# Input sums at every fifth place between matmuls, and wider steps in loading head outputs, in a two-layer decoder trunk

## The chip, the core and the metric

The kernel runs on one core of a Trainium2 chip. TensorE multiplies matrices into PSUM banks, VectorE, ScalarE and GpSimd work element by element, and SyncE issues the loads of the weights. The metric is the device time of one execution in microseconds, the median of three runs. Less is better.

## The reference, cut to what is computed

Two layers of a decoder trunk for 512 tokens of width 1024, all in float32:

```python
p      = x @ W_in        # retention q/k/v/gate, mLSTM q|k/v/o/i/f, two merge gates gA, gB
y_A    = P_A( swish(g_ret) * HeadNorm(Retention(q,k,v)) )
y_B    = P_B( sigmoid(o) * HeadNorm(mLSTM(conv(q),conv(k),v,i,f)) )
x      = LN(alpha * x + W_out( sigmoid(gA) * y_A + sigmoid(gB) * y_B ))
x      = LN(alpha * x + SwiGLU(x))
```

Retention and mLSTM have four heads each, with queries and keys of 128 columns and values of 256. The retention's score of two tokens is damped by their distance, its queries and keys are rotated by their position, and both branches normalise each head's output.

## The kernel before

**Numbers in two parts.** Each float32 operand is kept as a rounded part (`...h`, or `whi` for a weight) and the remainder that the rounding left (`...l`, `wlo`). A product is three matmuls: rounded by rounded, rounded by remainder, remainder by rounded. ScalarE makes the rounded parts (weights at L201), VectorE the remainders (`lo_of`, L133, for weights, values, scores and all else).

**Units.** The weights come in units of 512 KB, loaded by SyncE into `wraw`. A unit is 24 matmuls of 512 columns in the projections, or 24 of 256 columns in the quads, and its preparation runs up to four units ahead (`prep_to`, `used`). PSUM has four banks for projections (`pm`) and four for the rest (`pa`).

**The layer.** In a layer come two pairs of retention heads, two pairs of mLSTM heads, four quads (two for each merge gate), the branch outputs, W_out, the norm and SwiGLU. A retention pair (the loop over `p`, L665 on) is: four projections for queries and keys, each taken out of PSUM by a rotation (`rot_evac`: three VectorE products at L607 to L609, one GpSimd add at L610); the value projection, whose four banks become `rvh` on ScalarE and `rvl` on VectorE (`v_evac`); and the gate projection.

**Quads.** A quad makes four blocks of a projection from seven units instead of eight. It needs sums of weights (VectorE L187 to L191, GpSimd L223) and sums of blocks of the layer's input. `input_sums` (L571) makes the latter in four parts `m`: two GpSimd adds (L577) join rounded part and remainder of two blocks into a scratch tile `xs`, four VectorE operations (L583) fill a scratch tile `sf`, ScalarE rounds it to `xs0h` (L585; `xs1h` in layer 1), VectorE makes the remainder `xs0l` (L133). The results are not read before the quads.

**Work between matmuls.** TensorE's and SyncE's orders are written out by hand. Work beside the unit that is running is kept as generators in a queue `side`; `slot()` (L244) steps the first of them on and is called between matmuls (four times in a projection by units of features, sixteen in one by tokens, twice in a unit of a quad). For the second pair the queue holds the first pair's `head_norms` (which writes the head outputs `ot` to memory, `od`, at L543) during the rotations, and from then on the first head's `scores`, `input_sums`, and after the value projection `weighted`, the second head's `scores` and `weighted`. On VectorE, ScalarE and GpSimd a scheduler places the instructions; in the quads their order is as written, too.

**Head outputs.** `fetch` (L546) loads them back in four parts: GpSimd issues the load into a scratch tile `of` (L550), ScalarE rounds it to `orh` (L554), VectorE makes `orl`. The first `fetch` stands beside quads three and four, the second one (`om0h`, `om0l`) behind it, beside the next projection. All scratch tiles (`xs`, `sf`, `of`, `ot`, the quads' `ga` and `gc`, the scores' `pf` and `qf`) share four buffers.

Of the kernel before, what the change touches and what calls it, by code (L numbers as in the profile page):

```python
# [104 lines left out]
def decoder_trunk(ctx: ExitStack, tc: tile.TileContext, wall, xT_in, x_in, pvec, lnp, rtab, out):  # L105
# [18 lines left out]
    def scratch(shape, name):  # L124
        return reg.tile(shape, F32, tag="sc", name=name, bufs=4)

    def bigpair(which, name):
        h = big.tile([P, KT, S], F32R, tag=f"{which}h", name=f"{name}h")
        l = big.tile([P, KT, S], F32R, tag=f"{which}l", name=f"{name}l")
        return h, l  # L130

    def lo_of(out_lo, full, hi):
        nc.vector.tensor_tensor(out=out_lo, in0=full, in1=hi.bitcast(F32), op=ALU.subtract)  # L133
# [4 lines left out]
    for l in range(L):  # L138
        i = 0
        while i < NUNIT:  # L140
            n, m = len(loads), l * NUNIT + i
# [97 lines left out]
        prep_to(state["used"] + LOOK)  # L239


    side = deque()

    def slot():  # L244
        while side:
            try:
                next(side[0])
                return
            except StopIteration:
                side.popleft()  # L250

    def drain():
        while side:
            slot()
# [18 lines left out]
    def feat_if(xh, xl, evac):  # L273

        w = take()
        pm = main_bank()
        hi = w[0].rearrange("p (k m) -> p k m", k=KT)
        for k in range(KT):
            nc.tensor.matmul(pm, lhsT=hi[:, k], rhs=xh[:, k], start=(k == 0), stop=False)
            nc.tensor.matmul(pm, lhsT=hi[:, k], rhs=xl[:, k], start=False, stop=(k == KT - 1))  # L280
            if k % 4 == 3:
                slot()
        used()
        evac(pm)
# [119 lines left out]
    xh, xl = bigpair("A", "x0")  # L404
# [141 lines left out]
    def fetch(od, his, los):  # L546

        for i in range(4):
            t = scratch([P, 2, S], "of")
            nc.gpsimd.dma_start(t, od[:, 2 * i : 2 * i + 2])  # L550
            yield
            yield
            hi, lo = (x[i // 2][:, 2 * i % 4 : 2 * i % 4 + 2] for x in (his, los))
            nc.scalar.copy(hi, t)  # L554
            yield
            lo_of(lo, t, hi)
            yield
# [10 lines left out]
    def sum_views(which, name):  # L568
        return tuple(t.rearrange("p (s m) (c t) -> p s (m c) t", s=4, c=2) for t in bigpair(which, name))

    def input_sums(xh, xl, sh, sl):  # L571

        t1, t2 = slice(0, S // 2), slice(S // 2, S)
        for m in range(4):
            t = scratch([P, 2, S], "xs")
            for i in range(2):
                nc.gpsimd.tensor_tensor(out=t[:, i], in0=xh[:, m + 4 * i].bitcast(F32), in1=xl[:, m + 4 * i].bitcast(F32), op=ALU.add)  # L577
            yield
            f = scratch([P, 4, S // 2], "sf")
            a11, a12, a21, a22 = t[:, 0, t1], t[:, 1, t1], t[:, 0, t2], t[:, 1, t2]  # L580
            for i, a, b, op in ((0, a21, a22, ALU.subtract), (1, f[:, 0], a11, ALU.subtract),
                                (2, a11, a21, ALU.subtract), (3, f[:, 1], a12, ALU.add)):
                nc.vector.tensor_tensor(out=f[:, i], in0=a, in1=b, op=op)  # L583
            yield
            nc.scalar.copy(sh[:, :, m], f)  # L585
            lo_of(sl[:, :, m], f, sh[:, :, m])
            yield
# [5 lines left out]
    for l in range(L):  # L593
# [7 lines left out]
        xs = sum_views(oth, f"xs{l}")  # L601
        od = [dr.tile([P, KT, S], F32, tag=f"od{i}", name="od") for i in range(2)]

        def rot_evac(dst):
            def ev(pm):
                t = scratch([P, S], "rt")
                nc.vector.tensor_tensor(out=dst, in0=pm, in1=tab[:, 0], op=ALU.mult)  # L607
                nc.vector.tensor_tensor(out=t[0:64], in0=pm[64:128], in1=tab[0:64, 1], op=ALU.mult)
                nc.vector.tensor_tensor(out=t[64:128], in0=pm[0:64], in1=tab[64:128, 1], op=ALU.mult)  # L609
                nc.gpsimd.tensor_tensor(out=dst, in0=dst, in1=t, op=ALU.add)  # L610
            return ev
# [51 lines left out]
            yield  # L663

        for p in range(2):  # L665
            qk = reg.tile([P, 4, S], F32, tag="qk", name="rqk")
            rots = [rot_evac(qk[:, i]) for i in range(4)]
            if p == 0 and l > 0:
# [24 lines left out]
                return mult, key_weight, query_weight  # L693

            side.append(scores(qk, 0, boxes[0], *ret_weights(2 * p)))
            if p == 1:
                side.append(input_sums(xh, xl, *xs))
            if p == 0:
                side.append(rest(12))
                side.append(if_cols())  # L700
# [160 lines left out]

        ordered = {mybir.EngineType.Activation, mybir.EngineType.DVE, mybir.EngineType.Pool}
        with tc.manual_schedule(engines=ordered):
            for m in (0, 4):
                quad(xh, xl, *xs, gate_ev(sga, 0, m))
            drain()
            orh = [reg.tile([P, 4, S], F32R, tag=t, name="orh") for t in ("vh", "vl")]
            orl = [reg.tile([P, 4, S], F32R, tag=t, name="orl") for t in ("gt", "oo")]
            side.append(fetch(od[0], orh, orl))
            for m in (0, 4):  # L870
                quad(xh, xl, *xs, gate_ev(sgb, 8, m))
            drain()
# [245 lines left out]
        if not last:  # L1118
            xh, xl, _ = nxt
# [78 lines left out]
```

## Time and profile before

| what | value |
|---|---|
| median of three runs | 1806.07 us (1804.14 to 1806.31) |
| the profiled execution | 1806.1 us, of which the span is 1804.4 us |
| TensorE busy | 1772.4 us (98%) |
| VectorE busy | 1263.8 us (70%) |
| ScalarE busy | 794.3 us (44%) |
| GpSimd busy | 420.6 us (23%) |

The span runs from the first instruction to the last; busy times are shares of it. In the rows, PE is TensorE, DVE VectorE, ACT ScalarE, POOL GpSimd, SP SyncE, and L with a number is a line of the kernel before. A matmul's own time (0.39 us) overlaps the next one's: the step from start to start is what it costs. TensorE's clock is given as a share of its full speed, 1.00 being 2.4 GHz and 0.50 being 1.2 GHz.

### The profile page before, as it was taken

The numbers are of one execution on the slowest core, as the hardware profiler recorded it, in microseconds if no ns is written. First come the engines' busy times: TensorE is split into PE (matmuls) and PEld (weight loads), VectorE is DVE, ScalarE is ACT, GpSimd is POOL, SyncE is SP. The second block draws the span as 40 slices with busy tenths as digits, with TensorE's granted clock in tenths as the row PEclk, the third lists the DMA queues.
The fourth block names the chain that finished last, engine by engine and source line by source line (L and its number), as shares of the span: only waits on it lengthen the run. The fifth ranks groups of instructions, "written<-read, shape, count | busy, mean of one in ns | idle before, by whom it ended". The sixth has DMA issues, their size and how long they took to land.

```text
span 1804.4 us, 26440 instructions
## 1 busy us (share of the span) xinstructions
PE 1772.4 (98%) x10616; PEld 1580.5 (88%) x10616; DVE 1263.8 (70%) x1686; ACT 794.3 (44%) x1148; POOL 420.6 (23%) x309
## 2 busy tenths in 40 slices
PE   9998999999999999999999999999999999999997
PEld 7887888998889999988898788889988899999886
DVE  6676666775459999963476856667755599999534
ACT  4434655554225444452244345556532254444410
POOL 2041100231001455620120400012310015554200
PEclk9999999999999999999999999999999999999999
DMA  7332322247332333362243233213463333333521
GB/s 247 91 97 94 109 79 94 71 140 248 98 116 89 127 95 101 106 214 94 86 160 94 93 99 112 89 64 117 127 236 101 109 106 94 106 118 106 198 70 47
DMA packets 72826, 209.43 MB, mean 116 GB/s; under 512 B 6616, under 2 KB 8536, under 8 KB 71680
## 3 DMA queue, kind: packets, MB, share of 16 engines
q1 hardware_dynamic: 62864, 168.32, 29.0%
q0 software_dynamic: 9840, 39.43, 6.4%
q8 instruction: 83, 1.36, 0.3%
q14 instruction: 39, 0.32, 0.1%
HBM read 190.93 MB, written 16.79 MB: 115 GB/s over the span
## 4 chain that ended last, share of the span: by engine, by line
PE 92%; DVE 5%; issue 1%; ACT 1%; DMA 1%; POOL 0%; SPq 0%; DVEq 0%; ACTq 0%
PE pm L318 25%; PE pm L351 9%; PE pm L352 8%; PE pm L353 8%; PE pm L262 7%; PE pm L260 7%; PE pm L261 7%; PE pa L318 4%; PE pa L352 3%; PE pa L351 3%; PE pa L353 3%; DVE wlo L133 1%; DVE sf L583 1%; PE pa L484 1%; PE pa L485 1%; PE pa L486 1%
## 5 line engine op out<-in xcount | busy, mean ns | idle before, releaser
L133 DVE TENSOR_TENSOR wlo<-wraw,whi 128x1024 fp32r<-128x1024 f32 (+2 forms) x404 | 569.8, 1423 | 231.3 <-ACT whi L201 228.8
L201 ACT CAST whi<-wraw 128x1024 fp32r<-128x1024 f32 x391 | 408.8, 1049 | 507.2 <-PE pm L261 133.9
L440 POOL TENSOR_TENSOR rs<-ve,nhalf 128x4 f32<-128x4 f32 (+1 forms) x32 | 32.2, 1006 | 525.1 <-DVE ve L439 525.1
L351 PE MATMUL pm<-whi,x0h 128*128 128x512 f32 x256 | 102.9, 402 | 8.2 <-DVE rvl L133 8.1
L351 PE MATMUL pm<-whi,x20h 128*128 128x512 f32 x256 | 103.2, 403 | 7.0 <-DVE rvl L133 7.0
L353 PE MATMUL pm<-wlo,x20h 128*128 128x512 f32 x256 | 100.9, 394 | 0.0
L352 PE MATMUL pm<-whi,x20l 128*128 128x512 f32 x256 | 100.8, 394 | 0.0
L353 PE MATMUL pm<-wlo,x0h 128*128 128x512 f32 x256 | 100.7, 393 | 0.0
L352 PE MATMUL pm<-whi,x0l 128*128 128x512 f32 x256 | 100.5, 393 | 0.0
L223 POOL TENSOR_TENSOR wraw<-wraw 128x1024 f32<-128x1024 f32 x28 | 67.4, 2408 | 110.1 <-issue 54.4
L1049 POOL TENSOR_TENSOR qa<-qa 128x512 f32<-128x512 f32 x20 | 42.8, 2141 | 142.5 <-DVE qa L1048 90.6
L318 PE MATMUL pm<-s1h,wlo 128*128 128x256 f32 x240 | 67.9, 283 | 0.0
L318 PE MATMUL pm<-x10h,whi 128*128 128x256 f32 x240 | 67.9, 283 | 0.0
L318 PE MATMUL pm<-x10h,wlo 128*128 128x256 f32 x240 | 67.9, 283 | 0.0
L318 PE MATMUL pm<-s0h,whi 128*128 128x256 f32 x240 | 67.9, 283 | 0.0
L318 PE MATMUL pm<-x11h,whi 128*128 128x256 f32 x240 | 67.9, 283 | 0.0
L318 PE MATMUL pm<-x10l,whi 128*128 128x256 f32 x240 | 67.9, 283 | 0.0
L318 PE MATMUL pm<-s0l,whi 128*128 128x256 f32 x240 | 67.9, 283 | 0.0
L318 PE MATMUL pm<-x11l,whi 128*128 128x256 f32 x240 | 67.9, 283 | 0.0
L318 PE MATMUL pm<-s1h,whi 128*128 128x256 f32 x240 | 67.9, 283 | 0.0
L318 PE MATMUL pm<-s0h,wlo 128*128 128x256 f32 x240 | 67.9, 283 | 0.0
L318 PE MATMUL pm<-x11h,wlo 128*128 128x256 f32 x240 | 67.9, 283 | 0.0
(511 smaller groups left out, 5573.3 us busy)
## 6 DMA issues: line engine op xcount, KB each, us to landing
wraw<-wall SPq DMA_DIRECT2D x307, 512.0 KB, 3.7
od<-ot POOLq DMA_DIRECT2D x16, 512.0 KB, 3.0
of<-od POOLq DMA_DIRECT2D x16, 512.0 KB, 4.9
gb<-lnp POOLq DMA_DIRECT2D x4, 1024.0 KB, 6.5
x1d<-xr POOLq DMA_DIRECT2D x8, 512.0 KB, 2.9
xr<-x1d POOLq DMA_DIRECT2D x8, 512.0 KB, 4.7
negm<-md POOLq DMA_DIRECT2D x2, 1026.0 KB, 7.1
xr<-xtok POOLq DMA_DIRECT2D x4, 512.0 KB, 6.6
```

What stands on the lines that cost most here:

```text
L133: nc.vector.tensor_tensor(out=out_lo, in0=full, in1=hi.bitcast(F32), op=ALU.subtract)
L201: nc.scalar.copy(hi, sum_t[i])
L223: nc.gpsimd.tensor_tensor(out=raw_t[u + 2], in0=raw_t[u], in1=raw_t[u + 3], op=ALU.add)
L260: nc.tensor.matmul(pm[:, c0:c1], lhsT=hi[:, k], rhs=xh[:, k, c0:c1], start=(k == 0), stop=False)
L261: nc.tensor.matmul(pm[:, c0:c1], lhsT=hi[:, k], rhs=xl[:, k, c0:c1], start=False, stop=False)
L262: nc.tensor.matmul(pm[:, c0:c1], lhsT=lo[:, k], rhs=xh[:, k, c0:c1], start=False, stop=(k == KT - 1))
L318: nc.tensor.matmul(pm, lhsT=x[:, j, k], rhs=y[:, k], start=go and n == 0, stop=j == 1 and k == 3 and n == 2, skip_group_check=not first)
L351: nc.tensor.matmul(pm, lhsT=sh(k)[:, a], rhs=hi[:, j], start=first, stop=False)
L352: nc.tensor.matmul(pm, lhsT=sl(k)[:, a], rhs=hi[:, j], start=False, stop=False)
L353: nc.tensor.matmul(pm, lhsT=sh(k)[:, a], rhs=lo[:, j], start=False, stop=last)
L440: nc.gpsimd.tensor_tensor(out=rs[:, :n], in0=ve[:, :n], in1=nhalf[:, :n], op=ALU.pow)
L1049: nc.gpsimd.tensor_tensor(out=v, in0=v, in1=u, op=ALU.subtract)
```

## The change

A second queue, `slow`, is stepped on at every fifth call of `slot()`. `input_sums` goes into it at the start of the second pair, ahead of the rotations, and no longer into `side` behind the first head's scores. One step within a part of the sums is joined with the one behind it. In `fetch` one more step lies between load and rounding, and one more between rounding and remainder: a part takes six steps instead of four.

```diff
-    side = deque()
+    side, slow = deque(), deque()
+    SLOW = 5
+    turn = {"n": 0}
 
     def slot():
+        turn["n"] += 1
+        if slow and turn["n"] % SLOW == 0:
+            if next(slow[0], "end") == "end":
+                slow.popleft()
         while side:
...
             nc.gpsimd.dma_start(t, od[:, 2 * i : 2 * i + 2])
             yield
             yield
+            yield
             hi, lo = (x[i // 2][:, 2 * i % 4 : 2 * i % 4 + 2] for x in (his, los))
             nc.scalar.copy(hi, t)
+            yield
             yield
             lo_of(lo, t, hi)
             yield
...
                 nc.vector.tensor_tensor(out=f[:, i], in0=a, in1=b, op=op)
-            yield
             nc.scalar.copy(sh[:, :, m], f)
             lo_of(sl[:, :, m], f, sh[:, :, m])
             yield
...
         for p in range(2):
+            if p == 1:
+                slow.append(input_sums(xh, xl, *xs))
             qk = reg.tile([P, 4, S], F32, tag="qk", name="rqk")
...
             side.append(scores(qk, 0, boxes[0], *ret_weights(2 * p)))
-            if p == 1:
-                side.append(input_sums(xh, xl, *xs))
```

An `assert not slow` ahead of the quads is the only other line. In the changed program the lines of `input_sums` stand 8 further down (L577 is L585, L583 is L591), those of `rot_evac` and of the quads 7 (L610 is L617, L843 is L850, L853 is L860), that of the write of head outputs 6 (L543 is L549). What the two programs have in a row, by engine:

GpSimd in layer 0, from the first pair's norms (`rs`) to the end of the second pair's rotations (`rqk`) and the sums' adds (`xs`), before:

```order
L440 TENSOR_TENSOR rs<-ve,nhalf 128x4 x2
L610 TENSOR_TENSOR rqk<-rqk,rt 128x512 x2
L543 DMA od<-ot 128x1024
L610 TENSOR_TENSOR rqk<-rqk,rt 128x512
L543 DMA od<-ot 128x1024
L610 TENSOR_TENSOR rqk<-rqk,rt 128x512
L577 TENSOR_TENSOR xs<-x0h,x0l 128x512 x8
```

GpSimd at the same place, in the changed program:

```order
L446 TENSOR_TENSOR rs<-ve,nhalf 128x4
L585 TENSOR_TENSOR xs<-x0h,x0l 128x512 x2
L446 TENSOR_TENSOR rs<-ve,nhalf 128x4
L617 TENSOR_TENSOR rqk<-rqk,rt 128x512
L585 TENSOR_TENSOR xs<-x0h,x0l 128x512
L617 TENSOR_TENSOR rqk<-rqk,rt 128x512
L585 TENSOR_TENSOR xs<-x0h,x0l 128x512
L549 DMA od<-ot 128x1024
L617 TENSOR_TENSOR rqk<-rqk,rt 128x512
L549 DMA od<-ot 128x1024
L617 TENSOR_TENSOR rqk<-rqk,rt 128x512
L585 TENSOR_TENSOR xs<-x0h,x0l 128x512 x4
```

The first two parts' four adds moved ahead of the third rotation, four stayed behind the fourth; the writes of head outputs keep their places among the rotations, with four adds ahead of them. In layer 1 the first part's two adds stand ahead of the first rotation, the second part's ahead of the third, four behind the fourth.

VectorE in layer 0, the end of the way to the first values' remainders (`rvl`), before:

```order
L583 TENSOR_TENSOR sf<-sf,xs 128x256
L583 TENSOR_TENSOR sf<-xs 128x256
L583 TENSOR_TENSOR sf<-sf,xs 128x256
L133 TENSOR_TENSOR wlo<-wraw,whi 128x1024
L583 TENSOR_TENSOR sf<-xs 128x256
L133 TENSOR_TENSOR xs0l<-sf,xs0h 128x4x256
L583 TENSOR_TENSOR sf<-sf,xs 128x256
L583 TENSOR_TENSOR sf<-xs 128x256
L583 TENSOR_TENSOR sf<-sf,xs 128x256
L133 TENSOR_TENSOR wlo<-wraw,whi 128x1024
L133 TENSOR_TENSOR xs0l<-sf,xs0h 128x4x256
L133 TENSOR_TENSOR rvl<-pm,rvh 128x512 x3
```

VectorE at the same place, in the changed program:

```order
L591 TENSOR_TENSOR sf<-xs 128x256 x2
L591 TENSOR_TENSOR sf<-sf,xs 128x256
L591 TENSOR_TENSOR sf<-xs 128x256
L591 TENSOR_TENSOR sf<-sf,xs 128x256 x2
L591 TENSOR_TENSOR sf<-xs 128x256
L591 TENSOR_TENSOR sf<-sf,xs 128x256
L133 TENSOR_TENSOR xs0l<-sf,xs0h 128x4x256
L133 TENSOR_TENSOR wlo<-wraw,whi 128x1024
L133 TENSOR_TENSOR xs0l<-sf,xs0h 128x4x256
L133 TENSOR_TENSOR wlo<-wraw,whi 128x1024
L133 TENSOR_TENSOR rvl<-pm,rvh 128x512 x3
```

All four parts stood between the fourth rotation and `rvl`; now the first part stands ahead of the fourth rotation, the second part's VectorE work right behind that rotation, and the last two, shown here, where they were. In layer 1 the last part goes behind `rvl`, among the second head's scores.

VectorE in the fourth quad, from the third quad's last take-out (`ga`, L853) on, before:

```order
L853 TENSOR_TENSOR ga<-pm,ga 128x512
L133 TENSOR_TENSOR orl<-of,orh 128x1024
L133 TENSOR_TENSOR wlo<-wraw,whi 128x1024 x4
L843 TENSOR_TENSOR gc<-ga,pm 128x512
L133 TENSOR_TENSOR wlo<-wraw,whi 128x1024
L846 TENSOR_TENSOR ga<-pa,ga 128x512
```

VectorE at the same place, in the changed program:

```order
L860 TENSOR_TENSOR ga<-pm,ga 128x512
L133 TENSOR_TENSOR wlo<-wraw,whi 128x1024
L133 TENSOR_TENSOR orl<-of,orh 128x1024
L133 TENSOR_TENSOR wlo<-wraw,whi 128x1024 x3
L850 TENSOR_TENSOR gc<-ga,pm 128x512
L133 TENSOR_TENSOR orl<-of,orh 128x1024
L133 TENSOR_TENSOR wlo<-wraw,whi 128x1024
L853 TENSOR_TENSOR ga<-pa,ga 128x512
```

One weight's remainder moved ahead of `orl`, and the last `orl`, which was the one behind `ga`, now stands behind the take-out `gc`.

## Rows read from the trace of the kernel before

**Rows 1.** Waits of PE: engine tile line <- releaser: us in total, times, longest

```profile
PE pm L351 <- DVE rvl L133: 15.1, 4, 6.4
PE pa L318 <- DVE wlo L133: 2.8, 2, 1.7
```

**Rows 2.** Timeline of PE: start, us, engine, line, what, [idle before <- releaser]

```profile
140.39 0.39 PE L352 MATMUL pm<-whi,x0l 128*128 128x512 f32 x1
140.62 0.39 PE L353 MATMUL pm<-wlo,x0h 128*128 128x512 f32 x1
147.39 0.79 PE L351 MATMUL pm<-whi,x0h 128*128 128x512 f32 x1 [6.38 <-DVE rvl L133]
...
150.96 0.40 PE L351 MATMUL pm<-whi,x0h 128*128 128x512 f32 x1
...
1032.74 0.39 PE L353 MATMUL pm<-wlo,x20h 128*128 128x512 f32 x1
1039.51 0.80 PE L351 MATMUL pm<-whi,x20h 128*128 128x512 f32 x1 [6.38 <-DVE rvl L133]
...
1044.76 0.40 PE L351 MATMUL pm<-whi,x20h 128*128 128x512 f32 x1
```

**Rows 3.** A window (PE, PEld, DVE, ACT, POOL busy; PEclk; DMA; GB/s), a chain piece

```profile
147.00:148.00 1.00, 0.61 (x2) 0.52 (x3) 1.00 (x3) 1.00 (x2) 0.00 (x0) 0.50 0.76 287
...
577.62 11.52 PE pm L318 x96
```

**Rows 4.** Timelines of DVE, layers 0 and 1, and of POOL (last row)

```profile
119.82 1.23 DVE L133 TENSOR_TENSOR wlo<-wraw,whi 128x1024 fp32r<-128x1024 f32 x1
...
124.07 1.51 DVE L583 TENSOR_TENSOR sf<-xs 128x256 f32<-128x256 f32 x1
...
142.18 1.21 DVE L133 TENSOR_TENSOR xs0l<-sf,xs0h 128x1024 fp32r<-128x1024 f32 x1
143.31 0.41 DVE L583 TENSOR_TENSOR sf<-sf,xs 128x256 f32<-128x256 f32 x1
...
146.65 1.28 DVE L133 TENSOR_TENSOR rvl<-pm,rvh 128x512 fp32r<-128x512 f32 x2
...
1038.78 1.88 DVE L133 TENSOR_TENSOR rvl<-pm,rvh 128x512 fp32r<-128x512 f32 x3
...
119.88 2.31 POOL L610 TENSOR_TENSOR rqk<-rqk,rt 128x512 f32<-128x512 f32 x1 [3.38 <-DVE rt L609]
```

**Rows 5.** Windows of layer 0: L583 on DVE, then all engines

```profile
119.80:146.70 26.90, 11.57 (x16) 0.94 0.21 61
...
66.00:117.00 51.00, 51.00 (x261) 43.21 (x260) 27.21 (x54) 21.79 (x38) 10.14 (x7) 1.00 0.29 89
```

**Rows 6.** Timelines of DVE and PE in layer 1, second head's keys

```profile
1061.18 0.35 DVE L473 SCALAR_TENSOR_TENSOR pp<-pa,pv,pp 128x128 fp32r<-128x128 f32 x1 [0.43 <-ACT pp L472]
...
1062.92 0.28 PE L486 MATMUL pa<-rvh,pp 128*128 128x256 f32 x1
```

**Rows 7.** Timelines in layer 0's fourth quad; page: DMA issues, KB, us to landing

```profile
403.71 1.05 ACT L201 CAST whi<-wraw 128x1024 fp32r<-128x1024 f32 x1 [4.74 <-PE pm L318]
...
407.28 1.05 ACT L554 CAST orh<-of 128x1024 fp32r<-128x1024 f32 x1
...
404.66 0.68 DVE L853 TENSOR_TENSOR ga<-pm,ga 128x512 f32<-128x512 f32 x1
408.36 1.23 DVE L133 TENSOR_TENSOR orl<-of,orh 128x1024 fp32r<-128x1024 f32 x1 [3.02 <-ACT orh L554]
...
404.88 2.39 POOL L223 TENSOR_TENSOR wraw<-wraw 128x1024 f32<-128x1024 f32 x1 [1.86 <-issue]
...
410.77 0.39 PE L318 MATMUL pa<-xs0h,wlo 128*128 128x256 f32 x1 [1.05 <-DVE wlo L133]
...
od<-ot POOLq DMA_DIRECT2D x16, 512.0 KB, 3.0
of<-od POOLq DMA_DIRECT2D x16, 512.0 KB, 4.9
```

More of the change, by code (lines that the diff above doesn't have):

```diff
@@ L863, in decoder_trunk @@
         with tc.manual_schedule(engines=ordered):
+            assert not slow
             for m in (0, 4):
```

## The prediction, made blind

> **What bounds the kernel now.** I read the waits of TensorE first, because TensorE is the only engine that is nearly always at work. Its whole list is short, and two groups of it touch the change [rows 1]: four waits of the matmuls behind a value projection for the values' remainder `rvl` (15.1 us in all, the longest 6.4) and two waits in the quads for a weight's remainder `wlo` (2.8 us in all, the longest 1.7). Everything else on TensorE is matmuls back to back, so the change can only give back these waits, or make new ones. The timeline of TensorE then shows where they lie. In layer 0 the last matmul of the second pair's value projection starts at 140.62 and the next one, due 0.23 us later (the step from 140.39 to 140.62), starts at 147.39; in layer 1 the same two stand at 1032.74 and 1039.51 [rows 2]. Each is a gap of 6.54 us beyond the normal step, and after each the granted clock is at 0.50, the lower level of 1.2 GHz [rows 3].
>
> **What a gap costs with its tail.** In layer 0 the six 512-column and six 256-column matmuls from 147.39 to 150.96 take 3.57 us [rows 2]. At the higher level they take 6 x 0.23 + 6 x 0.12 = 2.10 (0.12 from 96 matmuls in 11.52 us, [rows 3]). The tail is 1.47 us and the gap with its tail 8.0 us. In layer 1 nine and six matmuls take from 1039.51 to 1044.76, 5.25 us against 9 x 0.23 + 6 x 0.12 = 2.79; tail 2.46, together 9.0 us. So 17.0 us lie in the two places.
>
> **Why the gap is there.** Before it VectorE has no idle time: from the last rotation (its first following instruction starts at 119.82) to the first `rvl` at 146.65 it works through weight remainders, the first head's scores and all four input sums [rows 4]. The 16 subtractions of L583 take 11.57 us of that stretch [rows 5], 0.72 each, though one takes 0.41 alone (143.31); the one at 124.07 takes 1.51 [rows 4]. The long ones run while GpSimd makes the sums' adds (L577). So a GpSimd add costs VectorE about 1.1 us (1.51 - 0.41), and there are eight adds in the stretch. It also goes the other way: the rotation's add at 119.88 takes 2.31 us beside a weight remainder at 119.82 that takes its usual 1.23 [rows 4]; there GpSimd waited, not VectorE.
>
> **The sums, layer 0.** A sum is two adds on GpSimd, four subtractions and one remainder on VectorE, and one rounding copy on ScalarE. In the changed order the first sum goes wholly before the fourth rotation, the second keeps its VectorE part behind it, but its two adds go before; the third and fourth stay where all were. The stretch loses on VectorE 4 x 0.41 + 1.21 = 2.85 us (the 1.21 is the `xs0l` remainder at 142.18, [rows 4]), and four adds at 1.1 = 4.4 us of waiting. Against that, the rotation's add now meets the second sum's short subtractions in place of one long weight remainder, so VectorE may wait 1.1 us there. Given back: 2.85 + 4.4 - 1.1 = 6.15. The first `rvl` then starts at 146.65 - 6.15 = 140.5, and TensorE 0.74 after it, as now (147.39 - 146.65): 141.24, against 140.85 due. 0.4 us of gap stay. The bounds: 7.25 without that wait (no gap), and 2.85 if no add's wait is saved; then `rvl` starts at 143.8, a gap of 3.7 us and a tail of at most the 1.5 seen now, 5.2 us lost. I take 0.4, because the waits of 1.1 us are read from rows of this very stretch.
>
> The Trainium skill ("SBUF — State Buffer", section "SBUF: two separate sides") says that VectorE and GpSimd share a pair of ports as an exclusive lock: the one that starts first holds it for its whole instruction and "the other fully blocks"; for a VectorE operation without a faster mode this holds if both inputs lie in SBUF. The rows on 1.51 against 0.41 agree. By this rule moved adds cost their lock again wherever they go, so it speaks against a gain from moving them.
>
> Whether they cost it there depends on how full the new place is. In the stretch from 66 to 117 us VectorE works 27.21 of 51 us and GpSimd 10.14 [rows 5]. What comes in there is one sum on VectorE (2.85), four adds (two sums) and their waits (4.4), and a rounding copy: 7.3 us into 23.8 idle ones. So I cost it at nothing. If that cover were gone, the rotations would come late by as much as 7.3 us, with the scores' matmuls behind them. ScalarE's copy of the first sum stands ahead of a weight copy and of the head outputs' copies; a unit of 24 matmuls lasts 24 x 0.23 = 5.5 us, ScalarE works 21.79 of the 51 [rows 5], and the copy of that shape takes 1.05 [rows 7].
>
> **The sums, layer 1.** Here the first sum goes before the fourth rotation and the fourth goes behind the values, into the gate projection; the adds of the third and fourth stay. The stretch loses 8 x 0.41 + 2 x 1.21 = 5.7 us and 4.4 us of waits. The first `rvl` would start at 1038.78 - 10.1 = 1028.7; it has to start by 1032.97 - 0.74 = 1032.2, so nothing of the gap stays (at the bound of 5.7 alone it starts at 1033.1, 0.9 us late). The fourth sum's 2.85 us now stand between the second head's scores, whose key remainder ends at 1061.18 + 0.35 = 1061.53; the matmul that reads it starts at 1062.92 [rows 6]. Slack 1.4 us, and VectorE idles there between its pieces (0.43 before this very one). Cost between 0 and 2.85 - 1.4 = 1.45 us; I take 0.1.
>
> **The head outputs' loads.** In the fourth gate quad the place of the wait is the weight remainder of its fifth unit. ScalarE has that weight rounded at 403.71 + 1.05 = 404.76, and VectorE is free from 404.66 + 0.68 = 405.34; but in VectorE's order the remainder `orl` of the fourth head output comes first, and waits 3.02 us for its copy on ScalarE (407.28 + 1.05). It runs from 408.36 for 1.23, the weight remainder behind it, and TensorE goes on at 410.77 after 1.05 us idle [rows 7]. In layer 1 the same wait is the longer of the two, 1.7 [rows 1]. With the wider steps the weight remainder stands ahead of that `orl`, so it can start at about 405.4; behind GpSimd's weight sum (2.39 us from 404.88) at the latest at 407.3, to end at 408.5, a good microsecond before it is due. Both waits go: 2.8 us. Bounds: nothing, if something else is late there, to 2.8.
>
> **Sum.** 17.0 - 0.4 - 0.1 + 2.8 = 19.3 us. The profiled execution took 1806.1 us, of which the span is 1804.4; its time is that of the median, 1806.07. So 1806.1 - 19.3 = 1786.8 us. With every term at its best bound 1786.3, at its worst 17.0 - 5.2 - 0.9 - 1.45 = 9.4, 1796.7.
>
> **Rivals.** (a) VectorE's waits for GpSimd come back in layer 0: the moved adds meet VectorE beside the earlier rotations, these come late, and the four adds that stay cost as much as the eight do now. Then only the 2.85 are given back and half of the gap stays. For it speaks that my sum ends within 0.4 us of the due time, with no slack, and that three sums still have their VectorE part ahead of `rvl`; against it the 23.8 idle us of the new place. Time: 1786.8 + (5.2 - 0.4) = 1791.6. It is also what the Trainium skill's rule on the lock ("SBUF — State Buffer", as above) gives where the new place is full.
>
> (b) The wider steps make a new wait behind the fourth quad. Two loads of the second head output now stand behind the fourth load of the first one on GpSimd, and the second of them needs the buffer that the fourth `orl` gives free. The fourth load is issued behind GpSimd's weight sum, at 404.88 + 2.39 = 407.3; with 4.9 to land, a copy of 1.05 and a remainder of 1.23 [rows 7] its `orl` ends at 414.5. The load behind it lands at 419.4, and ScalarE, which takes that copy ahead of the sigmoid that frees a bank of the quad, is held to about 420.5. The bank is wanted by the third unit of the projection behind the quads. TensorE's fifth unit of the quad starts at 410.77; three units of 24 x 0.12 = 2.9 and two of 5.5 later it is 430.5. So it should fit by 10 us. If something on the way is later than these rows say, I price it at the 3 us that `orl` waits now, in each layer, with the 2.8 not gained: 1786.8 + 2.8 + 6 = 1795.6.
>
> (c) Slower. The second sum of layer 0 takes over a buffer from which a head output is written out, and that write is now issued behind more adds on GpSimd, at the latest behind the third rotation's add: a unit of 5.5 us before 119.88 + 2.31 [rows 4], so at 116.7. It lands 3.0 later [rows 7], at 119.7, just ahead of the fourth rotation's last piece. VectorE works in order: if the write lands later, every instruction behind, `rvl` among them, is late by as much. To lose the 19.3 us and 3.6 more each layer must lose 11.5, so it decides from a write that lands at about 131, nearly five times as long as the writes take. Time then: 1812 (each layer 12.5 us late).
>
> (d) The change does not do what it says: TensorE's and SyncE's orders are the same in both programs, only VectorE, ScalarE and GpSimd are re-ordered. If the adds simply wait for buffers and run where they ran, 1803 to 1806.
>
> **How the numbers follow.** A measurement here can tell about 0.2%, 3.6 us, from no change. The forecast has 0.62 (1784.4 to 1789), (a) 0.18, (b) 0.09, (d) 0.06, (c) 0.05. The range reaches from the best bound, 1786.3, less the 1.9 us by which the fastest run shown (1804.14) lies under the median, over (a) with as much to spare on its side: 1784.4 to 1793.5; outside it are (c), (d) and most of (b). Faster by over 0.2%: 0.62 + 0.18 + 0.09 = 0.89; within 0.2%: 0.06; slower: 0.05.
>
> **What would show it.** Right: no wait of TensorE for `rvl` above 1 us in the second pair, no stretch of half clock behind it, no wait in the fourth gate quad; the first `rvl` of layer 0 at about 140.5 and of layer 1, relative to its value projection, some four microseconds before its due time; L583 at a mean well under 0.72 in layer 0. Wrong: `rvl` of layer 0 beyond 142 while VectorE stays without idle time, which is (a); a wait of TensorE in the projection behind the quads, (b); a wait of VectorE's L583 for a write to memory, (c).

## The result, and the profile after

The changed kernel takes 1786.17 us (median of four runs, 1784.78 to 1788.28) against 1805.43 us before (four runs, 1804.14 to 1806.31). The ratio is 0.9895 with an interval of 0.9878 to 0.9912: 1.05% faster. The prediction was 1786.8 us in a range from 1784.4 to 1793.5. The profiled execution has a span of 1786.6 us against 1804.4.

The waits of TensorE in the changed kernel, its whole list (the engine, the tile and the line that waited, what it waited for, us in total, times, the longest):

```profile
PE pm L357 <- DVE rvl L133: 2.3, 2, 1.7
PE pm L344 <- ACT whi L429: 2.3, 1, 2.3
PE pm L401 <- DVE nhalf L403: 1.1, 1, 1.1
PE pm L345 <- DVE wlo L133: 1.0, 2, 0.8
PE pa L667 <- DVE rows L658: 0.2, 1, 0.2
```

Of the four waits for `rvl` in [rows 1] the two long ones are gone; the two that stay are those of the first pairs. The waits of the quads for a weight's remainder (2.8 us in [rows 1]) are gone, and no new group has come.

The timeline of TensorE at the two places of [rows 2], layer 0 and layer 1:

```profile
143.46 0.39 PE L359 MATMUL pm<-wlo,x0h 128*128 128x512 f32 x1
143.69 0.40 PE L357 MATMUL pm<-whi,x0h 128*128 128x512 f32 x1
...
145.79 0.40 PE L357 MATMUL pm<-whi,x0h 128*128 128x512 f32 x1
...
1026.32 0.39 PE L359 MATMUL pm<-wlo,x20h 128*128 128x512 f32 x1
1026.55 0.39 PE L357 MATMUL pm<-whi,x20h 128*128 128x512 f32 x1
...
1028.64 0.40 PE L357 MATMUL pm<-whi,x20h 128*128 128x512 f32 x1
```

The step over the former gap is 0.23 us in both layers, where it was 6.77. From the last matmul of the value projection (143.46) to the one at 145.79 it is 2.33 us, against 10.34 for the same matmuls before (140.62 to 150.96): 8.0 us less in layer 0. In layer 1 the stretch from 1026.32 takes 2.32 us to 1028.64; before, the matmul that answers to the last one started at 1043.52, and the half clock went on to 1044.76 (1029.34 in the changed kernel), so that 9.0 us are saved to there.

The timeline of VectorE on the way to the first `rvl` in layer 0, then that `rvl` in layer 1, then GpSimd's add of the fourth rotation:

```profile
122.67 1.85 DVE L591 TENSOR_TENSOR sf<-xs 128x256 f32<-128x256 f32 x2
...
129.17 0.72 DVE L700 TENSOR_TENSOR qf<-rqk,rtab 128x256 f32<-128x256 f32 x1
129.82 2.31 DVE L133 TENSOR_TENSOR wlo<-wraw,whi 128x1024 fp32r<-128x1024 f32 x1
...
132.78 1.53 DVE L133 TENSOR_TENSOR pp<-qf,pp 128x256 fp32r<-128x256 f32 x1
134.23 1.85 DVE L591 TENSOR_TENSOR sf<-xs 128x256 f32<-128x256 f32 x2
...
142.76 1.88 DVE L133 TENSOR_TENSOR rvl<-pm,rvh 128x512 fp32r<-128x512 f32 x3
...
1023.35 0.68 DVE L133 TENSOR_TENSOR rvl<-pm,rvh 128x512 fp32r<-128x512 f32 x1
...
122.73 1.51 POOL L617 TENSOR_TENSOR rqk<-rqk,rt 128x512 f32<-128x512 f32 x1 [3.40 <-DVE rt L616]
```

The stretch from the fourth rotation to `rvl` takes 142.76 - 122.67 = 20.09 us, where it took 146.65 - 119.82 = 26.83 [rows 4]: 6.74 less. The four rows with 1.85 (two operations), 2.31 and 1.53 are those that a GpSimd add held up by 1.1 us: the rotation's add at 122.67, the sums' adds in the other three. TensorE needs `rvl` started by 143.69 - 0.74 = 142.95; it starts 0.2 us before that.

The window of that stretch with L591 (which was L583) alone; columns as in [rows 5]:

```profile
122.67:142.76 20.09, 6.45 (x12) 1.00 0.24 66
```

Twelve operations at a mean of 0.54 us, where sixteen had 0.72.

The fourth quad of layer 0 on VectorE, then ScalarE, then GpSimd's sum of weights:

```profile
397.75 0.68 DVE L860 TENSOR_TENSOR ga<-pm,ga 128x512 f32<-128x512 f32 x1
398.35 3.12 DVE L133 TENSOR_TENSOR wlo<-wraw,whi 128x1024 fp32r<-128x1024 f32 x1
401.39 1.21 DVE L133 TENSOR_TENSOR orl<-of,orh 128x1024 fp32r<-128x1024 f32 x1
...
416.06 0.83 ACT L840 ACTIVATE sgb<-pm,pv 128x256 f32<-128x256 f32 x2
...
397.97 2.41 POOL L223 TENSOR_TENSOR wraw<-wraw 128x1024 f32<-128x1024 f32 x1 [3.59 <-issue]
```

VectorE goes on without idle time where it waited 3.02 us [rows 7]. The weight remainder takes 3.12 us, since it meets the sum of weights, and is still in time.

**Where the time went.** Both programs give TensorE the same 10616 matmuls in the same order, so the start of each can be set against the start of its twin. The difference, after less before, changes at these places only:

| place | change of the difference, us |
|---|---|
| layer 0, first 62 us | +1.3 |
| layer 0, first pair, behind its own wait for `rvl` | +1.5 |
| layer 0, second pair: gap 6.5, half clock 1.5 | -8.0 |
| layer 0, fourth quad | -1.3 |
| layer 1, second pair: gap 6.5, half clock 2.5 | -9.0 |
| layer 1, quads: 0.4 ahead of the fourth, 2.0 in it | -2.4 |
| sum | -17.9 |

The two spans differ by 17.8. The first two rows are no work of the change, which does nothing before the second pair. They are the clock; those 1.3 us lie in the first 21 us. The windows of the kernel before (as rows 3: PE, PEld, DVE, ACT, POOL busy; PEclk; DMA; GB/s):

```profile
5.00:35.00 30.00, 27.28 (x106) 21.34 (x106) 18.49 (x32) 13.54 (x23) 3.09 (x2) 0.94 0.80 280
...
62.00:75.00 13.00, 12.23 (x67) 10.65 (x68) 7.93 (x18) 3.03 (x7) 0.01 (x1) 1.00 0.37 110
```

and of the changed one:

```profile
5.00:35.00 30.00, 26.67 (x100) 20.83 (x100) 17.13 (x30) 13.37 (x23) 3.09 (x2) 0.89 0.77 270
...
62.00:75.00 13.00, 11.26 (x55) 9.58 (x56) 7.67 (x14) 3.71 (x8) 0.54 (x1) 0.87 0.28 82
```

In the profile of after the granted clock of the first 35 us is 0.89 for 0.94, and the wait of 1.7 us in the first pair, which both kernels have, is followed by half clock in one and not in the other (0.87 for 1.00). Behind the first pair the two profiles differ by 8.0 + 1.3 + 9.0 + 2.4 = 20.7 us. All but the 0.4 ahead of layer 1's fourth quad (see the second run) is the change.

### The profile page after: what moved, and what is told of

Same layout as the page of the kernel before. It is cut to its first block, busy times and chain, and to the rows that moved or that the text cites. A ratio compares the mean times of both kernels' runs of the same rounds, so it can differ in the third digit from the quotient of the medians.

```text
span 1786.6 us, 26435 instructions
## 1 busy us (share of the span) xinstructions
PE 1769.7 (99%) x10616; PEld 1579.3 (88%) x10616; DVE 1269.8 (71%) x1686; ACT 795.4 (45%) x1148; POOL 415.6 (23%) x309
## 4 chain that ended last, share of the span: by engine, by line
PE 95%; DVE 3%; issue 1%; ACT 1%; DMA 1%; SPq 0%; DVEq 0%
PE pm L324 27%; PE pm L357 9%; PE pm L359 9%; PE pm L358 9%; PE pm L268 7%; PE pm L266 7%; PE pm L267 7%; PE pa L324 5%; PE pa L358 3%; PE pa L357 3%; PE pa L359 3%; PE pa L490 1%; PE pa L491 1%; PE pa L492 1%; PE pa L546 1%
## 5 line engine op out<-in xcount | busy, mean ns | idle before, releaser
L133 DVE TENSOR_TENSOR wlo<-wraw,whi 128x1024 fp32r<-128x1024 f32 (+2 forms) x404 | 579.2, 1445 | 230.1 <-ACT whi L201 227.0
L324 PE MATMUL pm<-s1l,whi 128*128 128x256 f32 x240 | 67.9, 283 | 0.0
```

The source lines that it names most:

```text
L324: nc.tensor.matmul(pm, lhsT=x[:, j, k], rhs=y[:, k], start=go and n == 0, stop=j == 1 and k == 3 and n == 2, skip_group_check=not first)
```

## Experiments

**Each part alone.** The first run keeps the sums' new places and takes the old steps in loading; the second does the opposite.

```diff
 # e1_sums_only, against the changed kernel
             nc.gpsimd.dma_start(t, od[:, 2 * i : 2 * i + 2])
             yield
             yield
-            yield
...
             nc.scalar.copy(hi, t)
             yield
-            yield
             lo_of(lo, t, hi)
```

> The input sums go at every fifth place, the loading of head outputs keeps its old steps. Theory (two separate gains that add up): both gaps before rvl in the second pairs are gone, the waits in the fourth gate quads (1.05 and 1.71 us before) stay: 8.0 us less in layer 0, 9.1 less in layer 1, so about 17 us under the kernel before, ratio 0.9905. Rival (the two parts share the gain, since both put off VectorE work): the waits in the quads go too, or part of a gap comes back, and the time is within 1 us of the whole change (ratio 0.9895) or over 0.993.

Measured: 1788.3 us (four runs) against 1804.77, ratio 0.9900 (0.9887 to 0.9913). Its waits of TensorE, the first two groups:

```profile
PE pa L324 <- DVE wlo L133: 2.4, 2, 1.6
PE pm L357 <- DVE rvl L133: 2.3, 2, 1.7
```

The waits in the quads are back (2.4 us, 2.8 before) and the two gaps are gone. Matmul against matmul, the second pairs give 8.0 and 9.0 us. The theory holds, the rival falls.

The second run has the fetch of the changed kernel in the kernel before:

```diff
 # e2_fetch_only, against the kernel before
             nc.gpsimd.dma_start(t, od[:, 2 * i : 2 * i + 2])
             yield
             yield
+            yield
...
             nc.scalar.copy(hi, t)
+            yield
             yield
             lo_of(lo, t, hi)
```

> Only the wider steps in loading head outputs. Theory: the gaps before rvl stay at 6.4 us idle each, the waits in the two fourth gate quads go, 1.2 us in layer 0 and 2.3 in layer 1, so 3.5 us less, ratio 0.998. Rival (the weight remainder is late there for another reason, and only moves): no wait of TensorE gone, ratio 1.000; or a new wait of TensorE in the projection behind the quads, ratio above 1.

Measured: 1801.65 us (twelve runs) against 1804.77, ratio 0.9983 (0.9973 to 0.9993). The group of the waits that stays:

```profile
PE pm L351 <- DVE rvl L133: 15.1, 4, 6.4
```

There is no wait of a quad left, both gaps stand as before, and the fourth quads give 1.3 and 2.0 us, with the 0.4 ahead of the second. That 0.4 is not the steps' doing: it is gone in the first and the third run, too, which keep the old steps. In the profile of before a head output came later there (ScalarE waits 4.33 us for the load ahead of its copy at 1280.82, and 3.80 in the first run). The changed kernel differs from the first run by the steps alone, and beside it they are worth 1.0 us in layer 0 and 1.9 in layer 1. Behind layer 1's gap this profile loses 0.9 us less to the half clock than that of before, after the same wait of 6.4 us.

The two parts add up: 0.9900 x 0.9983 = 0.9883, against 0.9895 (0.9878 to 0.9912) for both.

**What GpSimd's adds cost VectorE.** The third run leaves the adds out of the kernel before, and with them the remainders' part of the sums:

```diff
 # e3_no_adds, against the kernel before
-            t = scratch([P, 2, S], "xs")
-            for i in range(2):
-                nc.gpsimd.tensor_tensor(out=t[:, i], in0=xh[:, m + 4 * i].bitcast(F32), in1=xl[:, m + 4 * i].bitcast(F32), op=ALU.add)
             yield
             f = scratch([P, 4, S // 2], "sf")
-            a11, a12, a21, a22 = t[:, 0, t1], t[:, 1, t1], t[:, 0, t2], t[:, 1, t2]
+            x0, x1 = xh[:, m].bitcast(F32), xh[:, m + 4].bitcast(F32)
+            a11, a12, a21, a22 = x0[:, t1], x1[:, t1], x0[:, t2], x1[:, t2]
```

> The kernel before without the eight GpSimd adds per layer that join rounded part and remainder; the sums are made from the rounded part alone, so GpSimd's share of the work is left out and VectorE's stays in number and place. Theory (each add holds VectorE up by 1.1 us, eight of them 8.8 us): VectorE reaches the first rvl of layer 0 some 8.7 us earlier, both gaps of 6.5 us are gone with their tails, 17 us less than before, ratio 0.9905, and the operations of L583 take 0.41 each. Rival (VectorE's own work alone fills the stretch, its long operations only wait for data): at most 1 or 2 us of each gap go, ratio 0.997 to 1.000.

Measured: 1788.69 us (four runs) against 1804.77, ratio 0.9902 (0.9889 to 0.9915). VectorE in layer 0, the first of the sixteen operations, then the last way to `rvl`:

```profile
125.79 0.42 DVE L581 TENSOR_TENSOR sf<-x0h 128x256 f32<-128x256 f32 x1
...
139.13 1.23 DVE L133 TENSOR_TENSOR wlo<-wraw,whi 128x1024 fp32r<-128x1024 f32 x1 [0.90 <-ACT whi L201]
...
141.41 1.28 DVE L133 TENSOR_TENSOR rvl<-pm,rvh 128x512 fp32r<-128x512 f32 x2
```

From the fourth rotation (122.44 here) to `rvl` it is 18.97 us with 0.90 idle, against 26.83 without that idle time (both stretches have another 0.17 idle, which the prediction left out): VectorE works 8.8 us less, with its own work unchanged. That is 1.1 us for each of the eight adds, and the operation that took 1.51 [rows 4] takes 0.42. Without the adds neither gap stands.

**How full the new place is.** The fourth run puts the sums further apart, the fifth closer together:

```diff
 # e4_every_eighth / e5_every_second, against the changed kernel
-    SLOW = 5
+    SLOW = 8    # e4
+    SLOW = 2    # e5
```

> The whole change, with every eighth place in place of every fifth: in both layers two of the four sums now go behind the values' remainders, into the gate projection. Theory (a place with idle VectorE takes a sum for nothing): the first rvl of layer 0 comes at least 3 us before it is due instead of 0.2, the gate projection shows no wait of TensorE above 0.3 us, time within 1.5 us of the whole change, ratio 0.9895 with 0.001 to either side. Rival (the second head's scores have only 1.4 us of slack, a second sum there does not fit): TensorE waits for the second head's scores or their keys by 1 to 3 us in each layer, with a stretch of half clock behind it, 3 to 8 us more than the whole change, ratio 0.991 to 0.994.

Measured: 1787.13 us (four runs) against 1804.77, ratio 0.9894 (0.9881 to 0.9906): by time no difference from the whole change. The trace tells more. In layer 0's gate projection, TensorE, then VectorE, then GpSimd:

```profile
160.49 0.39 PE L490 MATMUL pa<-rvh,pp 128*128 128x256 f32 x1 [0.67 <-ACT pp L478]
...
155.79 1.52 DVE L591 TENSOR_TENSOR sf<-sf,xs 128x256 f32<-128x256 f32 x1
157.24 1.51 DVE L591 TENSOR_TENSOR sf<-xs 128x256 f32<-128x256 f32 x1
...
155.70 2.77 POOL L585 TENSOR_TENSOR xs<-x0h,x0l 128x512 f32<-128x512 f32 x2
```

Two adds hold up two subtractions among the second head's scores (1.5 us each). The sum's rounding on ScalarE waits for these, and the piece of the scores that TensorE needs (`pp`, L478) stands behind that rounding in ScalarE's order. Against the kernel before, 1.1 us are lost there in layer 0 and 1.2 in layer 1; the profile's total is nevertheless low, because its first 35 us ran at full clock (1.00). Neither expectation hit in full: the theory had the time but was wrong that nothing is lost, and the rival named the place but 3 to 8 us in all for 2.3.

> The whole change, with every second place in place of every fifth: in layer 0 all four sums now stand ahead of the fourth rotation's end, between the rotations, where VectorE had 23.8 idle us of 51 before; four sums with their waits for GpSimd are 4 x 2.85 + 8 x 1.1 = 20.2 us. Theory (VectorE's idle time there takes them): no wait of TensorE for rvl in the second pairs, none in the projections ahead of them above 0.3 us, time within 1 us of the whole change, ratio 0.9895 with 0.001 to either side. Rival (the place is nearly full, so rotations or weight remainders come late, and the projections wait for a bank or a weight): waits of TensorE between 66 and 125 us, 2 to 6 us in each layer, ratio 0.992 to 0.996.

Measured: 1797.94 us (five runs) against 1805.3, ratio 0.9963 (0.9949 to 0.9976): two thirds of the gain are gone. The rival was right, and a little too small: 7.0 us more than the whole change in layer 0 and 5.9 in layer 1, for 2 to 6. A wait that no other kernel here has:

```profile
PE pm L357 <- DVE rt L616: 8.3, 2, 4.1
```

VectorE, one rotation and the next with a sum between:

```profile
109.44 0.69 DVE L615 TENSOR_TENSOR rt<-pm,rtab 64x512 f32<-64x512 f32 x1
...
110.86 1.22 DVE L133 TENSOR_TENSOR wlo<-wraw,whi 128x1024 fp32r<-128x1024 f32 x1
112.00 1.84 DVE L591 TENSOR_TENSOR sf<-xs 128x256 f32<-128x256 f32 x2
113.77 0.87 DVE L591 TENSOR_TENSOR sf<-sf,xs 128x256 f32<-128x256 f32 x2
...
115.76 1.23 DVE L133 TENSOR_TENSOR xs0l<-sf,xs0h 128x1024 fp32r<-128x1024 f32 x1 [0.52 <-ACT xs0h L592]
117.02 0.69 DVE L615 TENSOR_TENSOR rt<-pm,rtab 64x512 f32<-64x512 f32 x1
```

From one L615 to the next it is 7.6 us, and a unit of TensorE lasts 5.5. A unit brings VectorE a rotation (2.1 us) and a weight's remainder (1.2), so 2.2 us are free in it; a sum takes 2.85 and its waits for GpSimd. With a sum in every unit VectorE falls behind by 2 us in each, the fourth rotation frees its bank late, and the value projection waits 4.1 us, with half clock behind (0.50 from 126.00 to 127.50). Most of VectorE's idle time lies ahead of the rotation at 99 us, where its order has the first of the four sums only (78.70 to 84.8).

**Is it VectorE's list?** The seventh run makes one remainder of the third sum three times:

```diff
 # e7_two_remainders_more, against the changed kernel
-            lo_of(sl[:, :, m], f, sh[:, :, m])
+            for _ in range(3 if m == 2 else 1):
+                lo_of(sl[:, :, m], f, sh[:, :, m])
```

> The whole change, with the third sum's remainder computed three times in place of once: 2.3 us more of VectorE ahead of rvl in both layers (the same values again). Theory (rvl is bound by VectorE's list; it is 0.2 us ahead of its due time in layer 0, 2.5 in layer 1): a wait of TensorE for rvl of about 2.0 us in layer 0's second pair, with up to 1.5 us of half clock behind it, none above 0.3 us in layer 1; 2 to 3.5 us more than the whole change, ratio 0.9906 to 0.9915. Rival (what is bound is something else, such as ScalarE's rounding of the values, and VectorE has spare time): no wait above 0.5 us, ratio 0.9895.

Measured: 1790.16 us (four runs) against 1805.3, ratio 0.9914 (0.9901 to 0.9928). The wait in layer 0:

```profile
144.18 0.71 PE L357 MATMUL pm<-whi,x0h 128*128 128x512 f32 x1 [1.93 <-DVE rvl L133]
```

1.93 us for an expected 2.0, none in layer 1, and 1.6 us of half clock behind it. The slack read from the profile, 0.2 us in layer 0 and over 2 in layer 1, is real.

**One step instead of two.** The eighth run has the first of the two new steps only:

```diff
 # e8_one_step_more, against the changed kernel
             nc.scalar.copy(hi, t)
             yield
-            yield
             lo_of(lo, t, hi)
```

> The whole change, but with one of the two new steps in loading head outputs (the one between load and rounding). VectorE's order in the fourth quad then again has a head output's remainder ahead of the weight remainder, now the third output's in place of the fourth's. Theory (what costs is that this remainder's load lands late): the third load has landed long before, VectorE does not wait for its rounding, and no wait of TensorE for a weight remainder stays in the quads. Rival (any head output's remainder ahead of the weight remainder makes it late): waits of about 1 and 1.7 us stay.

Measured: 1788.98 us, a single run, beside 1805.3, with TensorE waiting in both fourth quads, 1.5 us in layer 0 and 2.0 in layer 1. TensorE, then VectorE:

```profile
406.81 0.36 PE L324 MATMUL pm<-x0h,whi 128*128 128x256 f32 x1 [1.54 <-ACT om0h L561]
...
402.57 1.23 DVE L133 TENSOR_TENSOR orl<-of,orh 128x1024 fp32r<-128x1024 f32 x1 [0.66 <-ACT orh L561]
403.72 2.35 DVE L133 TENSOR_TENSOR wlo<-wraw,whi 128x1024 fp32r<-128x1024 f32 x2
405.99 0.68 DVE L849 TENSOR_TENSOR gc<-ga,pm 128x512 f32<-128x512 f32 x1
```

The profile names ScalarE's copy `om0h` as the releaser. By the program that matmul waits for two things, its weight's rounding and the bank that `gc` takes out, and `gc` ends at 405.99 + 0.68 = 406.67, 0.15 us before the matmul. In the trace of before a matmul at the same place in layer 1's third quad (1288.41) has only `gc` ending ahead of it, and it starts 0.15 us behind that end, too, while matmuls that wait for a ScalarE copy start 0.05 behind it; `om0h` ends at 406.81, together with the start. So it is VectorE's list again: with an `orl` ahead of it the weight's remainder is in time, but the take-out two instructions further on is late by as much. The theory was wrong that nothing waits, and the rival was about right on the size but not on the instruction. Matmul against matmul the two places cost 1.8 and 3.7 us, the second with half clock behind its wait, so with the first step alone nothing is gained there. Whether the second step alone would do, no run shows.

**The first pair's wait.** What stays of the waits for `rvl` is 1.7 us in layer 0's first pair and 0.6 in layer 1's. There VectorE works through the rows of the mLSTM gates. The sixth run gives three of its short copies to ScalarE:

```diff
 # e6_rows_on_scalar, against the changed kernel
-            nc.vector.tensor_copy(r1[0:4], r2[F])
+            nc.scalar.copy(r1[0:4], r2[F])
...
-            nc.vector.tensor_copy(r3[32:36], r0[0:4])
-            nc.vector.tensor_scalar(out=r2[0:4], in0=r2[0:4], scalar1=-1.0, scalar2=None, op0=ALU.mult)
+            nc.scalar.copy(r3[32:36], r0[0:4])
+            nc.scalar.activation(r2[0:4], r2[0:4], AF.Copy, scale=-1.0)
```

> The whole change, and three short copies of the mLSTM gates' rows (0.41 us each on VectorE, two of them right ahead of the first pair's rvl) moved to ScalarE, which waits there. Theory (the first pair's wait, 1.74 us in layer 0 and 0.6 in layer 1, has the cause that the second pair's had, VectorE's list ahead of rvl): the waits fall to about 0.9 and 0, so 1.4 us less, and less half clock behind them; ratio 0.988. Rival (the chain of the rows itself ends last, and a change of engine makes it longer): the wait of TensorE for the rows (0.2 us) grows by 0.5 to 1 us and the wait for rvl stays; ratio 0.9895 to 0.9905.

Measured: 1788.68 us (four runs) against 1805.3, ratio 0.9905 (0.9891 to 0.9918). TensorE's wait for `rvl`, then ScalarE:

```profile
PE pm L357 <- DVE rvl L133: 4.6, 2, 2.9
```

```profile
59.32 0.62 ACT L658 COPY rows<-rows 4x512 f32<-4x512 f32 x1 [3.56 <-DVE rows L657]
...
61.44 1.52 ACT L713 CAST rvh<-pm 128x512 fp32r<-128x512 f32 x3
```

The waits grew from 1.7 and 0.6 to 2.9 and 1.7. Now ScalarE waits 3.56 us for VectorE's rows, and the rounding of the values, in order behind it, comes at 61.44; in the changed kernel the first stood at 57.67. Neither expectation named this: the chain did not end last (TensorE's wait for the rows, 0.2 us, is gone), but what stood behind it in ScalarE's order did.

The ninth run takes two of the copies out instead, by writing where they would put it, and asks for the third later:

```diff
 # e9_short_rows, against the changed kernel
-                nc.vector.tensor_tensor_scan(out=r2[F, a], data0=r1[F, a], data1=r1[F, a], initial=0.0,
+                nc.vector.tensor_tensor_scan(out=r1[0:4, a], data0=r1[F, a], data1=r1[F, a], initial=0.0,
...
-            nc.vector.tensor_copy(r1[0:4], r2[F])
...
-            nc.vector.scalar_tensor_tensor(out=r0[0:4], in0=r1[0:4], scalar=-1.0, in1=r2[0:4], op0=ALU.mult, op1=ALU.subtract)
-            nc.vector.tensor_copy(r3[32:36], r0[0:4])
+            nc.vector.scalar_tensor_tensor(out=r3[32:36], in0=r1[0:4], scalar=-1.0, in1=r2[0:4], op0=ALU.mult, op1=ALU.subtract)
...
+            if p == 0:
+                side.append(rows_out())    # the sign of r2 and its write to memory
```

> The whole change, and two copies less in the chain of the mLSTM gates' rows: the sums run over the log forget gates and the row for the columns are written where the copies put them; the third short operation (the sign of the running maximum) is asked for later, though VectorE's order keeps it where it was. Theory (the first pair's wait is VectorE's list ahead of rvl, like the second pair's was): two operations of 0.41 us with their gaps, 0.9 us, leave the list; the wait of TensorE for rvl in the first pair falls from 1.74 to about 0.9 us in layer 0 and from 0.6 to nothing in layer 1, and nothing else changes: 1.4 us less than the whole change, ratio 0.9887. Rival (ScalarE's rounding of the values or the rows' chain ends last there): the waits stay at 1.74 and 0.6, ratio 0.9895.

Measured: 1783.62 us (four runs) against 1806.19, ratio 0.9869 (0.9853 to 0.9886). Its wait for `rvl`:

```profile
PE pm L357 <- DVE rvl L133: 1.0, 1, 1.0
```

1.7 and 0.6 have become 1.0 and nothing, as the theory has it (0.9 and nothing). Matmul against matmul, beside the repeated run below, layer 0 gains 1.0 us there and layer 1 0.6. Its median is the lowest of all.

The changed kernel once more, beside the ninth run:

> The whole change once more, beside the kernel before on the same chip as the run above. Both theories: ratio 0.9895 within 0.001; TensorE waits for rvl only in the first pairs, 1.74 and 0.6 us, none in the second pairs and none in the quads. What may differ from the profile shown is the clock in the first 75 us, where the time before the first second-pair rotation varied by up to 5 us between profiles of kernels that are equal up to there.

Measured: 1784.26 us (four runs) against 1806.19, ratio 0.9874 (0.9859 to 0.9888). Its waits for `rvl` are those of the first profile, 1.7 and 0.6 us, and there is none in the quads.

The ninth run is faster than it by 0.64 us, which the runs can't tell from nothing; its gain is read from the waits. This repetition is 1.9 us under the first measurement of the same kernel, and its profile is 3.06 us shorter: nearly all of that lies in the first 68 us, 1.4 before 62 and 1.5 behind the first pair's wait.

## Why the prediction was right, step by step

**The two gaps and their tails, 17.0 us.** Read from the timeline alone, they came out as 8.0 and 9.0. The granted clock behind a wait is worth counting: 1.5 and 2.5 us of the 17.0. It is no fixed price: the second run had the same wait in layer 1 and 0.9 us less behind it.

**Layer 0, 0.4 us of gap left.** Measured: none. The sum was 6.15 us given back, and 6.74 came. Its items were of the right kind: the rotation's add held up a short subtraction by 1.1 us (1.51 on GpSimd beside 1.85 for two on VectorE), four of the eight adds stayed. The 0.6 us on top come from those four: three held VectorE up by 1.1 us each, the first by 0.3 only (129.17, where 0.72 stands for the 0.42 of the third run). That add began at 128.12, and the operation right behind its start, which reads a PSUM bank, kept its 0.41 (128.38). The two ends that I gave, 2.85 and 7.25, enclose it, and `rvl` is in time by only 0.2 us, which the seventh run confirms. So it was close to rival (a), and this was not known from the sum, which had no room for 0.6 us of error.

**The lock.** That an add on GpSimd costs VectorE 1.1 us is shown by the third run, 8.8 us for eight. The rule of the Trainium skill ("SBUF — State Buffer", section "SBUF: two separate sides") agrees with it. That moved adds pay again in a new place is borne out by the fourth run, where two of them cost 1.1 us a layer and VectorE had little slack. That they pay wherever they go is not, as the next point shows.

**"I cost it at nothing".** Here the result was right and the reason was poor. I set 7.3 us against 23.8 idle ones in 51. The fifth run shows that this sum is of no use: idle time counts in the unit in which the work falls, 2.2 us in each with a rotation. The change got away with it because one sum and four adds are spread over the time up to the fourth rotation, and the rotations absorbed them without a wait. The four adds were cheap there, too. GpSimd's and VectorE's rows in the changed kernel, in order of time:

```profile
78.86 2.86 POOL L585 TENSOR_TENSOR xs<-x0h,x0l 128x512 f32<-128x512 f32 x2
81.11 0.89 DVE L700 TENSOR_TENSOR qf<-rqk,rtab 128x256 f32<-128x256 f32 x1
...
108.22 1.30 POOL L585 TENSOR_TENSOR xs<-x0h,x0l 128x512 f32<-128x512 f32 x1 [2.23 <-DVE sf L591]
109.20 1.41 DVE L133 TENSOR_TENSOR xs0l<-sf,xs0h 128x1024 fp32r<-128x1024 f32 x1 [0.52 <-ACT xs0h L592]
```

The first pair of adds lengthened two operations by 0.6 us together (0.89 for the 0.41 of before at 81.11, 0.70 for 0.56 at 79.87), the third add one by 0.2 (1.41 for 1.22), and the fourth, at 114.39, ran beside the rotation's products, which read a PSUM bank and kept their 0.69 and 0.68. That is 0.8 us for the 4.4 of the prediction. What it did not count is the rotation's own add at 104.56, which now meets two subtractions of the first sum (104.42, 1.85 for two, 1.1 us).

**Layer 1.** Nothing of the gap stayed, as said; `rvl` starts 2.5 us ahead of the latest point (1026.55 - 0.74 - 1023.35), where the sum gave 3.5. The fourth sum in the gate projection cost nothing (I took 0.1), with its adds made long before; where adds went along with it, in the fourth run, it did cost.

**Loading the head outputs, 2.8 us.** Measured 1.3 and 2.0, 3.3 us, in the whole change and in the second run, and 2.9 beside the first run; the 0.4 ahead of the second place is not theirs. The mechanism, VectorE waiting for a copy in order ahead of a weight's remainder, is shown by the rows of the fourth quad above, where it waits no more, and by the eighth run, in which half of the step moved the wait on by two instructions. Rival (b) did not come true; no wait of TensorE stands in the projection behind the quads. ScalarE's sigmoid was expected at 420.5 in the times of before, and it runs at 416.06, which is 422.5 there (the difference of the two traces is 6.4 us at that place). The load ahead of it took 6.8 us from its issue (408.29) to ScalarE's copy (415.10), for the 4.9 of the sum, and 8 of the 10 us of room stayed.

**Rivals (c) and (d).** L591 never waits for a write to memory in the changed kernel, and the adds run where the order has them (a pair at 78.86 already, 26 us before VectorE takes it up).

**The total.** 19.3 us were expected and the profiles differ by 20.7 behind the first pair, yet the forecast of 1786.8 meets the median of 1786.17 to 0.6. That is luck to the extent of 1 to 2 us. The terms were 1.4 too small: 0.5 for the losses that did not come, 0.5 in the fourth quads, and the 0.4 that is not the change's. The profile of after, of the slowest of the four executions (1788.28), lost 2.8 us more than that of before to the clock in its first 75 us. The terms as measured give 1806.1 - 20.7 = 1785.4; the first median lies 0.8 above it and the repetition's, 1784.26, 1.1 below.

## What to carry to other kernels

Where the engine that is always at work waits for another, read that other engine's list backwards from the wait: what stands in it and is not needed soon is the price, and so is each instruction that another engine's work makes longer. Before moving such work, count the free time of each unit at the new place, and not the idle share of a long stretch, and look at what it will run beside there: the same add cost VectorE 1.1 us beside subtractions and nothing beside the rotation's products. Count also what follows a wait at half clock, and look for the next instruction in the same list that becomes late.

## What was not expected of the hardware

The same 1.7 us of waiting in the first pair is followed by a stretch at 1.2 GHz in some profiles and not in others (granted 0.87 and 1.00 from 62 to 75 us), which is worth 1.4 to 1.5 us. In the first 35 us the granted clock was 0.89, 0.94 or 1.00 in profiles of kernels that do the same there. What decides this was not settled. Up to 75 us the profiles of kernels that do the same there differ by up to 4.8 us, and the two medians of the changed kernel by 1.9, so gains below that are read from the trace and not from the times.
